# Layer 0's modulation chunks 4 to 11: two weight blocks per step, four column strips together

## The chip, the core and the metric

One core of one Trainium2 chip runs the whole program. The metric is the device time of one execution in microseconds (us). The engines are named as in the profile: PE (TensorE, matmul), PEld (its weight loads), DVE (VectorE), ACT (ScalarE), POOL (GpSimd) and SP (SyncE, which here only issues DMAs). L326 is line 326 of the kernel before.

## The reference

A two-layer transformer trunk in float32 over 512 latent and 256 context tokens of width 1024. Per layer:

```
m  = silu(c) @ w_mod[l] + b_mod[l]          # 6 x 1024 columns, for the latent and the context condition
h  = rmsnorm(x) * g * (1 + m.scale1) + m.shift1
z  = h @ w_in[l]                            # q, k, v, gate u, value v of the gMLP
a  = attention(q, k, v)                     # 8 q heads, 2 kv heads; latent queries see 768 keys, context queries 256
g  = gelu(u) * spatial_mix(layernorm(gelu(v)))
x += m.gate1 * (concat(a, g) @ w_out[l])
x += m.gate2 * (relu(norm2(x) modulated by m.scale2, m.shift2 @ w_ff1[l])**2 @ w_ff2[l])
```

The part that the change touches is the first line for layer 0: two condition vectors (1024 numbers each) times a 1024 x 6144 matrix, in 12 chunks of 512 columns. Chunks 0 to 3 (shift 1 and scale 1) are needed before the first projection; chunks 4 to 11 (gate 1 and the three of the MLP) are needed only after the attention.

## The kernel before, in words

**Layout.** Activations lie feature-major: 128 features on the partitions, tokens along the free axis. Dense products are taken in three passes of fp32r matmuls on a high and a low part of each operand (`split`, L206 to L208: ACT writes the high part, DVE or POOL the low part). The many rows named L203 are all matmuls of the helper `mm`.

**Weight stream.** `block_order` (L120) writes down the order in which weight blocks of 128 x 1024 (512 KB) are used. `pump` (L224) walks this list and issues one DMA per block on SP while fewer than RING = 4 entries are live; `take` hands the oldest entry to its user, and `release` gives the entry back 4100 ns (REL) of the emission clock later. An entry of ordinary weights has a raw buffer (two of these) and a slot in each of two rings of four, "hi" and "lo". A modulation block is not split: it is loaded straight into a "hi" slot, and the "lo" slot that would belong to it stays unused.

**Modulation on PE.** `mod_chunk` (L315) makes one chunk of 512 columns out of 8 matmuls, one per 128 input features k. The stationary operand is `S32[:, k, :]`, 32 columns that repeat the two conditions; the moving operand is 512 columns of a weight block, in plain fp32, which the program runs as two passes (so one matmul is two records of L326). A matmul fills 32 of PE's 128 columns. With NS = 2 (chunks 0 to 3) the products alternate between two column strips; with 4 strips (chunks 4 to 11) feature k goes to strip k % 4, which is rows 32(k % 4) and on of one PSUM bank. A block holds two features, so a block's two matmuls are in strips 0 and 1 or in strips 2 and 3. The generator yields after each block. At the end DVE turns the bank (L334), and four small matmuls (L339) add the strips.

**Attention of layer 0.** `attention` runs first over the context queries (16 tiles of 128 queries of one head), then over the latent queries (32 tiles). A tile is: scores on PE into a `pa` bank (L203 `pa<-B,B`), maximum on DVE (L825), exponential on ACT (L828), transposes on PE (L844), copies of these by ACT (L846) and DVE (L847), and per two tiles the product with V (L203 `pb<-A,B`, 12 matmuls for latent tiles).

**Fillers.** After each tile's scores are emitted, `Flow.step` emits one piece of other PE work, the filler. In layer 0 the fillers are, in order: the pieces of chunks 4 and 5; then a mix of the first half of the output projection ("o" pieces, one of 8 output tiles x 2 token parts of 384, 12 matmuls each) and chunks 6 to 11 ("m" pieces, one weight block each) in the order of the string FILL0; then the second half of the output projection (`proj4(("out", l, 1), ...)`): 8 pieces of 12 matmuls over the 256 context tokens, which need the context heads, and 8 pieces of 12 matmuls over the 512 latent tokens, which need all heads. While the heads for a pass are not all emitted, that generator says "wait" and the step emits nothing.

**Order.** Two things set the order of work. `Flow` keeps an emission clock (`fl.vt`, in ns); what is put off (the transposes by T0, the V products by PV0, the freeing of ring entries by REL) is emitted when the clock gets there. A planner then orders each engine's instructions: of those that are ready in its plan, the one emitted first goes first. A row of matmuls that was emitted together can therefore be cut by an earlier-emitted piece of attention that becomes ready in between. Each engine runs its list strictly in order. In the first stage (`start`) PE and DVE keep the written order.

Of the kernel before, what the change touches and what calls it, by code (L numbers as in the profile page):

```python
# [16 lines left out]
KT = 8  # L17
# [8 lines left out]

# columns of the packed constants
PK1 = {"c": (0, 8), "cc": (8, 16), "bmod": (16, 112), "ng": (112, 144), "gn": (144, 152), "ident": (152, 280), "sel": (280, 312)}
PK2 = {"qg": (0, 64), "kg": (64, 128), "bs": (128, 640)}


# emission lags and periods, in ns of tensor-engine time
PAR = {"KF": 1, "XO": 1, "MS": 3, "KB": 6, "S0": 200.0, "S2": 1.0, "BK": 1, "CS": 0, "S1": 2400.0, "NS": 2, "CX": 0,
# [6 lines left out]


def once(fn):
    """fn, but for the first call alone"""
    left = [fn]
    return lambda: left.pop()() if left else None


class Flow:
    """Emission clock: counts tensor-engine time and emits put-off work once its turn has come."""

# [35 lines left out]
    def fill0(self, until):  # L86
        """pass the time without fillers"""
        while self.vt < until:
            self.vt = max(self.vt, min([until] + [e[0] for e in self.todo]))
            self.tick()  # L90

    def step(self):
        """one piece of filler"""
        while self.fillers:
            try:
                if next(self.fillers[0]) != "wait":
                    break
                return
            except StopIteration:
                self.fillers.pop(0)  # L100
        self.tick()

    def drain(self):
        """Emit everything put off, with fillers in between."""
        while self.todo:
            self.fill(self.todo[0][0] + 1e-6)
# [5 lines left out]

# how pieces of the output projection (o) and of the modulation (m) alternate beside the attention of layer 0
FILL0 = "oooooooommmommmmmmmmmommmmommmommmomoomo"
EARLY = [f"A{i}" for i in range(7, 3, -1)] + [f"B{i}" for i in range(7)] + ["C0", "C1"] + [f"A{i}" for i in range(7, 3, -1)]
# [4 lines left out]
def block_order():  # L120
    o = []
    mod = lambda j: [("mod", 0, j, kb) for kb in range(4)]
    tok = lambda l, g: [("tok", l, g, kb) for kb in range(2)]
# [37 lines left out]
def trunk(ctx: ExitStack, tc: tile.TileContext, xT, pk1, pk2, rope, wsT, w_mod, w_tok, w_u, w_out, w_ff1, w_ff2, outT):  # L161
# [47 lines left out]

# [1 line left out]
    order = block_order()  # L211
# [7 lines left out]
    def convert():  # L219
        """split the oldest block that is held back"""  # L220
        if held:
            split(*held.pop(0))

    def pump():  # L224
        while state["live"] < RING and state["pos"] < len(order):
# [10 lines left out]
            if early:  # L236
                raw = unit(early, [128, 1024], F32)
            elif key[0] == "mod":
                raw = ring.tile([128, 1024], F32, tag="hi", name=nm("hi"), bufs=RING)
            else:  # L240
                raw = ring.tile([128, 1024], F32, tag="raw", name=nm("raw"), bufs=2)
            nc.sync.dma_start(raw, src)
            if key[0] == "mod":
                ready.append((key, raw, None))
                state["pos"] += 1
                state["live"] += early is None
                continue
# [26 lines left out]
    def rsqrt(v, n):  # L274
        """1/sqrt of a small positive tile: a bit estimate, a quadratic and a cubic step."""
        yi = small(n, I32)
# [12 lines left out]

# [1 line left out]
    c1 = const.tile([128, 312], F32, name="c1")  # L291
# [9 lines left out]

    # silu of both conditions
    sc = const.tile([128, 8, 2], F32, name="silu")
# [11 lines left out]
    def mod_chunk(l, j, lag=1200.0):  # L315
        """512 columns of the modulation of both conditions, four partial sums at a time in the four
        32-column strips of the tensor engine; yields between weight blocks."""
        ps = pb()
        ns = PAR["NS"] if j < 4 else 4
        rows = ns * 32  # L320
        for kb in range(4):
            w = take("mod", l, j, kb)[0]
            for k2 in range(2):
                k = kb * 2 + k2
                q = (k % ns) * 32
                pe.matmul(ps[q:q + 32, :], S32[:, k, :], w[:, k2 * 512:(k2 + 1) * 512], start=k < ns, stop=k >= KT - ns)  # L326
            fl.vt += 490.0
            if l or j > 3:
                release()
            if kb < 3:  # L330
                yield
        # 32 by 32 blocks turned, then the strips added
        tr = (tw if l == 0 and j < 4 else tsm)([128, 512])
        vec.transpose(tr[0:rows], ps[0:rows])  # L334

        def fin():
            p4 = pt((128, 4, 2))
            for a in range(4):
                pe.matmul(p4[a * 32:a * 32 + 32], P1("sel")[0:rows], tr[0:rows].rearrange("p (m a i) -> p a m i", m=4, a=4)[:, a, :, 0:2], start=True, stop=True)  # L339
            mod_store(l, j, p4)  # L340
        if lag:
            fl.defer(lag, fin)
        else:
            fin()
        yield

    def mod_wide(l):
        """The modulation of one layer on the vector engine; yields after each half of a weight block."""
        raw = tk([128, 2, 512], F32)
# [6 lines left out]
        for j in range(12):  # L356
            acc = unit("C1", [128, 2, 512], F32)
            for k in range(KT):
# [15 lines left out]
                if k not in PAR["YK"]:  # L374
                    yield
            # sums over the partitions: 32 by 32 blocks turned and summed, then the four strips added
            part = small(32).rearrange("p (c b) -> p c b", c=2)
# [32 lines left out]

# [1 line left out]
    class Norm:  # L412
# [17 lines left out]
        def sums(self, *others):  # L430
            """1/rms of each token, for other chunks in the same go"""
            every = (self,) + others
# [50 lines left out]

# [1 line left out]
    class TokProj:  # L485
# [14 lines left out]
        def bank(self, tp):  # L500
            """256 tokens"""
            ps = (pt if self.early else pb)((128, 2, 256))
# [13 lines left out]
        def wide(self, ks=range(KT)):  # L516
            """the first 512 tokens, feature block by feature block as they come"""
            if 0 in ks:
# [11 lines left out]

# [1 line left out]
    DENSE = {0: ((0, 384), (384, 384)), 1: ((0, 512),)}  # L532
# [17 lines left out]
    def consts(l):  # L550
        k2 = const.tile([128, 640], F32, tag="k2", name=nm("k2"))
        nc.scalar.dma_start(k2, pk2[l])
        P2 = lambda k: k2[:, PK2[k][0]:PK2[k][1]]
        # rope tables times the gains
        cs = tw([128, 2, 4, 32])
        nc.scalar.dma_start(cs, rope)
        G = const.tile([128, 2, 2, 4, 64], F32, tag="G", name=nm("G"))
        for i, nme, s in ((0, "qg", HD ** -0.5), (1, "kg", 1.0)):
            g = P2(nme).rearrange("p (a b) -> p a b", a=2)
            vec.tensor_scalar_mul(g, g, s)  # L560
            for hf in range(2):
                gb = lambda a: g[:, a, :].unsqueeze(1).broadcast_to([128, 4, 32])
                vec.tensor_tensor(out=G[:, i, 0, :, hf * 32:hf * 32 + 32], in0=cs[:, 0], in1=gb(hf), op=ALU.mult)
                vec.scalar_tensor_tensor(out=G[:, i, 1, :, hf * 32:hf * 32 + 32], in0=cs[:, 1], scalar=(-1.0, 1.0)[hf], in1=gb(1 - hf), op0=ALU.mult, op1=ALU.mult)
        # spatial gating
        wr = ring.tile([128, 512], F32, tag="raw", name=nm("raw"), bufs=2)
# [9 lines left out]
    def layer(l, h, nxt, K, kv=None, kv0=0):  # L576
# [11 lines left out]
        def qk(ps4, tp, nh, which):  # L588
            """ps4 [128, 2, nh, 64] -> normed and rotated."""
            sq = tsm([128, 2, nh, 64])  # L590
# [28 lines left out]
        def turn(stk, tp, plan):  # L619
            """plan: (destination, [(head in stack, first column)]) -> transposes of both token tiles."""  # L620
            for dst, hs in plan:
# [46 lines left out]
        with region('kv%d' % l):  # L668
            kv.wide(range(kv0, KT))
        # gate path u, feature-major, twice its gelu  # L670
        U = [unit(f"C{i}", [128, 2, T], F32) for i in range(2)]
# [13 lines left out]
        def u_part(m, part):  # L685
            """one token part of a gate tile: first the noised tokens, later the context"""
            off, n = ((0, SEQ), (SEQ, CTX))[part]
# [89 lines left out]

        # residual update: x += gate * product, by condition
        def gate(i, m, off, n, src):
# [6 lines left out]
        def proj4(keys, R, i, passes, bank, post=None, gates=None):  # L786
            """keys: 4 blocks; passes: lists of token parts, each over all 8 output tiles."""
            wbs = {}
# [22 lines left out]

        # attention; the split output of a head pair takes the place of its queries
        def attn_tile(j, blk, hh, qt, st):
# [132 lines left out]

        # squared-ReLU MLP
        hslots = [f"B{i}" for i in range(7)] + ["C0"]
# [14 lines left out]
        def ff1_first():  # L963
            """first chunk, one token part after the other, while the other part is being normed"""
            wbs = [take("ff1", l, m) for m in range(4)]
# [197 lines left out]
```

## Time and profile before

| | |
|---|---|
| three runs | 1532.07, 1532.15 and 1535.47 us, median 1532.15 |
| profiled execution, first to last instruction (span) | 1530.9 us |
| what lies around the span | 1.25 us against the median run; the profiled execution has no other time of its own |
| PE busy | 1484.1 us, 97% of the span |
| DVE, ACT, POOL busy | 957.4, 682.6, 402.0 us |
| mean granted TensorE clock | 0.993 |
| matmuls of chunks 4 to 11 | first at 176.6 us, last at 341.0 us |
| context tiles, latent tiles of layer 0 | about 176 to 227 us, 227 to 345 us |
| first matmul of the first MLP product | 381.7 us |

Times are from the start of the span. "Busy" is the time covered by at least one instruction of the engine; matmuls are pipelined and their ends are modelled, so neighbouring matmul records overlap. In the timeline, a row gives the start, the time that the merged instructions cover, the engine, the line, the tiles (out<-in) and the count.

### The profile page before, as it was taken

How to read it: one execution, taken by the hardware profiler on the slowest of the kernel's cores; microseconds unless marked ns; L12 is line 12 of the kernel's file. 1: busy time of each engine (PE TensorE's matmuls, PEld its weight loads, DVE VectorE, ACT ScalarE, POOL GpSimd, SP SyncE). 2: the span in 40 equal slices, each digit the busy share in tenths (PEclk: the TensorE clock that was granted, in tenths of full speed). 3: DMA queues.
4: the chain of work that ended last, by engine and by line, in shares of the span. 5: the costliest groups of instructions: out<-in, count | busy, mean ns of one | idle time of the engine just before them, and what ended most of it. 6: DMA issues, size and time to landing. Idle time of an engine off the chain costs nothing.

```text
span 1530.9 us, 22786 instructions
## 1 busy us (share of the span) xinstructions
PE 1484.1 (97%) x8804; PEld 1321.5 (86%) x8804; DVE 957.4 (63%) x1874; ACT 682.6 (45%) x1142; POOL 402.0 (26%) x362
## 2 busy tenths in 40 slices
PE   6999899999999999999999999998999999999998
PEld 2899686779899999999999998996889888888887
DVE  5868966776855555555555547988796644444443
ACT  3542355564545453545444424535784433322221
POOL 0112320023244545545454603035213000000000
PEclk9999999999999999999999999999999999999999
DMA  9221324321134333333333321221101333332332
GB/s 359 67 74 48 119 91 152 110 83 56 62 108 122 113 123 126 111 118 106 124 109 124 98 68 56 86 80 44 41 1 56 97 96 97 98 97 97 96 98 79
DMA packets 49948, 148.83 MB, mean 97 GB/s; under 512 B 5424, under 2 KB 6832, under 8 KB 49840
## 3 DMA queue, kind: packets, MB, share of 16 engines
q1 hardware_dynamic: 49264, 146.46, 29.9%
q8 instruction: 69, 1.13, 0.3%
q10 hardware_dynamic: 576, 0.92, 0.2%
q14 instruction: 39, 0.32, 0.1%
HBM read 145.26 MB, written 2.10 MB: 96 GB/s over the span
## 4 chain that ended last, share of the span: by engine, by line
PE 82%; DVE 12%; DMA 2%; ACT 2%; issue 1%; POOL 0%; SPq 0%; ACTq 0%; POOLq 0%; DVEq 0%
PE pa L203 51%; PE pb L203 21%; PE pt L844 3%; PE pt L203 3%; PE pb L326 2%; DVE lo L208 1%; DMA X<-in_xT 1%; DMA C<-in_w_mod 1%; DVE X L784 1%; DMA A<-in_w_mod 1%; DVE m L277 1%; PE pt L626 1%; DVE B L961 1%; ACT hi L207 1%; PE pb L865 0%
## 5 line engine op out<-in xcount | busy, mean ns | idle before, releaser
L203 PE MATMUL pa<-A,hi 128*128 128x384 f32 (+2 forms) x1696 | 449.2, 347 | 1.7 <-ACT w L954 0.6
L207 ACT CAST hi<-raw 128x1024 fp32r<-128x1024 f32 x171 | 179.5, 1050 | 409.9 <-PE pa L203 326.3
L208 DVE TENSOR_TENSOR lo<-raw,hi 128x1024 fp32r<-128x1024 f32 x155 | 202.7, 1308 | 215.8 <-ACT hi L207 212.4
L203 PEld LDWEIGHTS pa<-A,hi 128*128 128x128 f32 x1696 | 304.7, 188 | 25.9 <-ACT w L954 1.8
L369 POOL TENSOR_TENSOR C<-C,s 128x512 f32<-128x512 f32 x168 | 240.5, 1463 | 245.0 <-ACT s L368 244.8
L203 PE MATMUL pa<-A,lo 128*128 128x384 f32 (+2 forms) x848 | 293.4, 347 | 1.1 <-DVE lo L208 1.1
L203 PE MATMUL pa<-B,hi 128*128 128x384 f32 (+1 forms) x900 | 246.4, 356 | 4.4 <-DVE X L784 4.4
L203 PEld LDWEIGHTS pa<-B,hi 128*128 128x128 f32 x900 | 162.9, 188 | 21.5 <-DVE X L784 9.2
L784 DVE SCALAR_TENSOR_TENSOR X<-pa,modT,X 128x384 f32<-128x384 f32 (+1 forms) x168 | 88.0, 547 | 143.0 <-PE pa L203 143.0
L203 PEld LDWEIGHTS pa<-A,lo 128*128 128x128 f32 x848 | 159.3, 188 | 12.0 <-DVE lo L208 1.3
L203 PE MATMUL pa<-B,lo 128*128 128x384 f32 (+1 forms) x450 | 158.1, 353 | 0.0
L203 PE MATMUL pb<-B,hi 128*128 128x256 f32 (+2 forms) x600 | 152.3, 340 | 0.4 <-DVE X L784 0.4
L368 ACT ACTIVATE s<-k,silu 128x512 f32<-128x512 f32 x168 | 114.3, 716 | 49.4 <-DMA k<-in_w_mod 27.3
L203 PE MATMUL pb<-hi,A 128*128 128x256 f32 x672 | 126.1, 285 | 0.0
L784 DVE SCALAR_TENSOR_TENSOR X<-pb,modT,X 128x512 f32<-128x512 f32 (+3 forms) x116 | 69.1, 602 | 75.8 <-PE pb L203 75.3
L203 PEld LDWEIGHTS pb<-B,hi 128*128 128x128 f32 x600 | 104.0, 189 | 11.6 <-DVE X L784 1.0
L203 PEld LDWEIGHTS pb<-hi,A 128*128 128x128 f32 x672 | 106.1, 191 | 0.2 <-issue 0.2
L203 PE MATMUL pb<-B,lo 128*128 128x256 f32 (+2 forms) x300 | 101.5, 338 | 0.0
L203 PE MATMUL pb<-lo,A 128*128 128x256 f32 x336 | 95.3, 284 | 0.0
L203 PEld LDWEIGHTS pa<-B,lo 128*128 128x128 f32 x450 | 84.4, 188 | 5.8
L847 DVE TENSOR_TENSOR A<-pt,A 128x384 fp32r<-128x384 f32 (+1 forms) x144 | 73.6, 535 | 16.4 <-ACT A L846 14.4
L846 ACT CAST A<-pt 128x384 fp32r<-128x384 f32 (+1 forms) x144 | 64.6, 469 | 43.3 <-PE pt L844 39.5
(169 smaller groups left out, 2300.3 us busy)
## 6 DMA issues: line engine op xcount, KB each, us to landing
raw<-in_w_ff SPq DMA_DIRECT2D x128, 512.0 KB, 3.5
k<-in_w_mod SPq DMA_DIRECT2D x96, 256.0 KB, 3.0
hi<-in_w_mod SPq DMA_DIRECT2D x32, 512.0 KB, 3.6
raw<-in_w_tok SPq DMA_DIRECT2D x19, 512.0 KB, 3.5
raw<-in_w_out SPq DMA_DIRECT2D x16, 512.0 KB, 3.5
A<-in_w_mod SPq DMA_DIRECT2D x8, 512.0 KB, 9.9
raw<-in_w_u SPq DMA_DIRECT2D x8, 512.0 KB, 3.5
B<-in_w_mod SPq DMA_DIRECT2D x6, 512.0 KB, 10.2
```

The source lines that it names most:

```text
L203: pe.matmul(out, a, b, start=start, stop=stop)
L207: act.copy(hi, src)
L208: (eng or vec).tensor_tensor(out=lo, in0=src, in1=hi.bitcast(F32), op=ALU.subtract)
L277: vec.tensor_scalar(yi, v.bitcast(I32), -0.5, 1595932665.0, op0=ALU.mult, op1=ALU.add)
L326: pe.matmul(ps[q:q + 32, :], S32[:, k, :], w[:, k2 * 512:(k2 + 1) * 512], start=k < ns, stop=k >= KT - ns)
L368: act.activation(p, w, AF.Copy, scale=s)
L369: pool_e.tensor_tensor(out=a, in0=a, in1=p, op=ALU.add)
L626: pe.transpose(p[:, o:o + 128], stk[:, t, hh, c0:c0 + 128].bitcast(F32), ident)
L784: vec.scalar_tensor_tensor(out=xs, in0=src[:, s - off:e - off], scalar=modT[l][:, i * 8 + m, cond:cond + 1], in1=xs, op0=ALU.mult, op1=ALU ...
L844: pe.transpose(tp_[:, (kt - k0) * 128:(kt - k0) * 128 + 128], p[:, kt * 128:kt * 128 + 128], ident)
L846: act.copy(pth[:, k0:k0 + step, d], src)
L847: vec.tensor_tensor(out=ptl[:, k0:k0 + step, d], in0=src, in1=pth[:, k0:k0 + step, d].bitcast(F32), op=ALU.subtract)
```

## The change

Chunks 4 to 11 take their weights two blocks at a time. One ring entry now holds two blocks, the first in the "hi" slot and the second in the "lo" slot, each by its own 512 KB DMA. A piece of `mod_chunk` is four matmuls, in strips 0 to 3, and a chunk has two pieces instead of four. The emission clock counts 260 ns for each matmul (1040 for four) where it counted 490 for a block of two; chunks 0 to 3 keep their two strips and one block per piece, but count 520. FILL0 has 12 "m" (one per pair of blocks) instead of 24, and the same 16 "o".

```diff
-FILL0 = "oooooooommmommmmmmmmmommmmommmommmomoomo"
+FILL0 = "oooooooomomomomomomomomommmm"
...
-    mod = lambda j: [("mod", 0, j, kb) for kb in range(4)]
+    mod = lambda j: [("mod", 0, j, kb) for kb in range(0, 4, 1 if j < 4 else 2)]
...
             elif key[0] == "mod":
-                raw = ring.tile([128, 1024], F32, tag="hi", name=nm("hi"), bufs=RING)
+                two = [ring.tile([128, 1024], F32, tag=t, name=nm(t), bufs=RING) for t in ("hi", "lo")]
+                for i in range(2):
+                    nc.sync.dma_start(two[i], w_mod[0, key[2], key[3] + i])
+                ready.append((key, *two))
+                state["pos"] += 1
+                state["live"] += 1
+                continue
...
             if key[0] == "mod":
                 ready.append((key, raw, None))
                 state["pos"] += 1
-                state["live"] += early is None
                 continue
...
         ns = PAR["NS"] if j < 4 else 4
         rows = ns * 32
-        for kb in range(4):
-            w = take("mod", l, j, kb)[0]
-            for k2 in range(2):
+        for kb in range(0, 4, ns // 2):
+            ws_ = take("mod", l, j, kb)[:ns // 2]
+            for k2 in range(ns):
                 k = kb * 2 + k2
-                q = (k % ns) * 32
-                pe.matmul(ps[q:q + 32, :], S32[:, k, :], w[:, k2 * 512:(k2 + 1) * 512], start=k < ns, stop=k >= KT - ns)
-            fl.vt += 490.0
-            if l or j > 3:
+                q = k2 * 32
+                pe.matmul(ps[q:q + 32, :], S32[:, k, :], ws_[k2 // 2][:, k2 % 2 * 512:(k2 % 2 + 1) * 512], start=k < ns, stop=k >= KT - ns)
+            fl.vt += PAR["MV"] * ns
+            if j > 3:
                 release()
-            if kb < 3:
+            if kb < 4 - ns // 2:
                 yield
```

`PAR` gains `"MV": 260.0`. Comments are taken out elsewhere, and nothing else changes.

2 rows, old and new, of the table PAR are left out of this document.

## The prediction

> **What bounds the kernel now.** I read the page first, then each engine's busy time by stage, then PE's rows of the stage in which chunks 4 to 11 run.
>
> ```profile
> span 1530.9 us, 22786 instructions
> PE 82%; DVE 12%; DMA 2%; ACT 2%; issue 1%; POOL 0%; SPq 0%; ACTq 0%; POOLq 0%; DVEq 0%
> ```
>
> PE holds 82% of the chain that ended last.
>
> ```profile
> core 0: us, PE busy (x) PEld busy (x) DVE busy (x) ACT busy (x) POOL busy (x), PEclk, DMA share, GB/s
> 176.00:227.00 51.00, 43.60 (x277) 34.36 (x275) 35.25 (x97) 26.74 (x72) 15.81 (x22) 0.93 0.41 136
> 187.00:193.00 6.00, 5.46 (x18) 2.98 (x16) 3.14 (x12) 2.19 (x8) 0.57 (x3) 0.53 0.05 21
> 227.00:345.00 118.00, 116.43 (x739) 83.01 (x737) 83.09 (x175) 67.89 (x150) 17.73 (x36) 1.00 0.35 112
> 345.00:364.00 19.00, 18.97 (x158) 18.73 (x157) 10.68 (x24) 8.58 (x20) 7.69 (x8) 1.00 0.17 56
> 364.00:382.00 18.00, 18.00 (x84) 14.74 (x83) 13.42 (x28) 6.94 (x12) 6.08 (x4) 1.00 0.17 59
> 1098.00:1140.00 42.00, 41.80 (x307) 37.98 (x305) 39.74 (x85) 37.45 (x87) 7.62 (x23) 1.00 0.00 1
> 1140.00:1150.00 10.00, 9.47 (x75) 8.61 (x73) 7.43 (x17) 6.30 (x16) 1.30 (x4) 1.00 0.01 2
> ```
>
> The context tiles of layer 0 are the first row, the latent tiles the third, what follows them the fourth and fifth. From 227 us on PE is covered 99% of the time, DVE 70%, ACT 58%. So a microsecond taken from PE between 227 and 382 us comes off the end, as long as another engine doesn't take PE's place. The context stage has 7.4 us in which PE is idle. The last two rows are layer 1's latent tiles without any filler, and what follows them; they serve below.
>
> **What the modulation costs.** The row is that of L326 from 176 to 382 us; the other rows are PE's timeline.
>
> ```profile
> L326 PE MATMUL pb<-hi,S 128*32 128x512 f32 x128 | 36.6, 612 | 0.9 <-DMA hi<-in_w_mod 0.9
> ```
>
> ```profile
> 227.80 1.05 PE L326 MATMUL pb<-hi,S 128*32 128x512 f32 x4
> ...
> 267.08 1.07 PE L326 MATMUL pb<-hi,S 128*32 128x512 f32 x8
> 268.08 0.55 PE L844 MATMUL pt<-c,w 128*128 128x128 f32 x3
> ...
> 283.94 1.04 PE L326 MATMUL pb<-hi,S 128*32 128x512 f32 x2
> 284.92 1.69 PE L203 MATMUL pb<-A,B 128*128 128x256 f32 x12
> 286.54 1.04 PE L326 MATMUL pb<-hi,S 128*32 128x512 f32 x2
> 287.52 0.96 PE L203 MATMUL pa<-B,B 128*128 128x512 f32 x4
> ...
> 340.99 1.05 PE L326 MATMUL pb<-hi,S 128*32 128x512 f32 x4
> ```
>
> A matmul is two records. At 283.94 one matmul alone holds PE for 0.98 us, until the next row starts at 284.92. At 267.08 four matmuls (two blocks that happened to meet, in strips 0 to 3) hold it for 1.00 us. One, two and four strips cost the same: the price is per group, 1.0 us. A group covers about 1.05 us, so the 36.6 us are 35 groups, for 64 matmuls. Sixteen full groups of four would do.
>
> The pair 283.94 and 286.54 is one block torn in two: after its first matmul a product with V, emitted earlier, had become ready and the planner put it between. From 227.80 to 340.99 there are 96 records in 28 groups: 15 of two matmuls, 11 of one, one of three, one of four. So 12 matmuls lost their partner, which is 6 torn blocks of 24, 0.25 per joint between two matmuls of a block.
>
> **The sum.** It is made against the span of 1530.9 us; the median run of 1532.15 is 1.25 us above it, and I carry this over unchanged.
>
> *Groups removed.* A group of four has three joints. With no tears there are 16 groups, 19 fewer: -19 us. With 0.25 tears at each joint there are 12 tears, 28 groups, 7 fewer: -7 us. A tear lets the waiting work through, so the next joint is less exposed than the first; but a piece of four also holds PE longer in the plan. I take the middle, 7 tears and 23 groups: 12 fewer, -12 us. One of these stood before 182 us, ahead of this idle stretch, where PE time is free:
>
> ```profile
> 186.64 0.69 PE L844 MATMUL pt<-c,w 128*128 128x128 f32 x2 [4.75 <-ACT w L828]
> ```
>
> That leaves -11 us, with ends -18 and -6.
>
> The four-strip price is a row of this kernel, but the Trainium skill speaks against it: "TensorE: Matmul & The Clock Gate", section "Part 3: Packing small matmuls — row/col tiling", gives 2.38 times for three column tiles, not 3. At that efficiency (0.79) a group of four would take 0.98/0.79 = 1.24 us, an estimate from that page, and the sixteen pieces would give back up to 3.8 us. The row at 267.08 (1.00 us) doesn't agree, and I go by the row.
>
> *Steps of filler.* There are 48 attention tiles and one piece per tile. Before, 8 pieces of chunks 4 and 5 plus 40 of FILL0 make exactly 48, and the second half's context pieces come behind the last tile. Now there are 4 + 28 = 32. So tiles 33 to 40 get the 8 context pieces of the second half, and tiles 41 to 48 get nothing ("wait"). PE's work is the same; its place is not.
>
> Bare tiles: the trace has them in layer 1. These are the exponentials, one per tile, from 227 to 345 and from 1098 to 1140 us.
>
> ```profile
> L828 ACT ACTIVATE w<-pa,m 128x768 f32<-128x768 f32 x31 | 28.1, 907 | 12.3 <-DVE m L825 10.6 <-DVE A L395 1.5
> L828 ACT ACTIVATE w<-pa,m 128x768 f32<-128x768 f32 x18 | 16.4, 910 | 1.2 <-DVE m L825 1.2
> ```
>
> Bare tiles take 42.0/18 = 2.33 us, with PE busy 2.32 and DVE 2.21 of it. So DVE stands just behind PE. In layer 0 DVE also makes the low part of the attention output, which layer 1 gives to POOL, and that could lift a tile to DVE's pace. I count 1 us for the eight tiles; the ends are 0 and 4 (0.5 us each).
>
> *The tail.* The eight context pieces covered the wait for the last tile.
>
> ```profile
> 347.77 0.40 PE L203 MATMUL pb<-B,hi 128*128 128x256 f32 x2
> ...
> 353.53 5.75 PE pb L203 x48
> ...
> 357.69 1.60 PE L203 MATMUL pb<-A,B 128*128 128x256 f32 x12
> ...
> 364.13 0.63 PE L203 MATMUL pb<-B,hi 128*128 128x512 f32 x2
> ```
>
> Matmuls over 256 columns go at 5.75/48 = 0.12 us, so the 96 of the context pieces are 11.5 us of the 16.4 between 347.77 and 364.13, where the latent pieces start. Without them PE waits for exponential, transposes, copies and V product. Layer 1 again shows that case:
>
> ```profile
> 1139.45 0.71 PE L203 MATMUL pa<-B,B 128*128 128x512 f32 x3
> ...
> 1148.45 0.49 PE L203 MATMUL pb<-B,hi 128*128 128x256 f32 x2
> ```
>
> From the last scores (ended 1140.16) to the second half 8.3 us pass, and PE is covered for 9.47 of the 10 us from 1140. Transposes and V products of the tiles before fill nearly all of it. I take 2 us lost (ends 0.5 and 11.5, all of the cover).
>
> *Weights.* The DMAs stay 32 of 512 KB for these chunks, now two per entry on SP's queue.
>
> ```profile
> hi<-in_w_mod SPq DMA_DIRECT2D x32, 512.0 KB, 3.6
> SPq L242 <- PE pb L326: 92.0, 22, 10.8
> PE pb L326 <- DMA hi<-in_w_mod: 0.9, 1, 0.9
> L207 ACT CAST hi<-raw 128x1024 fp32r<-128x1024 f32 x171 | 179.5, 1050 | 409.9 <-PE pa L203 326.3
> L208 POOL TENSOR_TENSOR lo<-raw,hi 128x1024 fp32r<-128x1024 f32 x4 | 9.6, 2394 | 5.5 <-ACT hi L207 5.5
> ```
>
> SP waits for PE to free slots, PE hardly for the data (0.9 us, once). Four entries now hold eight blocks, so a pair is fetched at least two steps (over 6 us) ahead of its use. If that cover were gone, a pair would cost PE about 3.6 us plus the second block's time; with all 16 pairs that is over 58 us, which I exclude because the slots free no later than before. Behind a waiting pair on SP stand the output blocks. The second half's four blocks are now wanted at tile 33, and each gets its slot from one of the last four pairs; after the slot it needs the cast (1.05 us) and the low part (2.39 us on POOL). The first has one slot freed at tile 29, so it is ready; if not, PE stands for at most 3.4 us. I count 0. In exchange the first half's blocks find free slots sooner in the context stage, which could fill up to 3 us of its idle time. Also 0.
>
> *Emission clock.* Chunks 0 to 3 add 30 ns 16 times in a stage with written order, and lags there are relative to later calls; 0, with a bound of 2 us either way for what the planner reshuffles. Vector transposes (L334) and strip sums (L339) stay eight each. Half as many releases cost no engine time.
>
> Sum: -11 + 1 + 2 = -8 us, so 1522.9 for the span and **1524.0** for the run.
>
> **The rivals.**
>
> *The groups stay whole.* Nearly every group in the timeline directly follows a tile's scores, so all four may be ready at once with nothing else pending. At most 2 tears: -17 or so, plus 2 for the tail: 1517. Against it speak the 6 torn blocks of 24.
>
> *The groups are torn as before* (the change doesn't do what it says). 28 groups or more, -6 after the hidden one, plus 3 for bare tiles and tail: -3, 1529, no measurable difference. For it: 0.25 tears per joint, three joints now.
>
> *The tail is bare.* One mechanism: the last tile's chain isn't shortened by the pieces' going, and PE idles 11.5 us before the latent pieces. An idle stretch also costs clock: after the 4.75 us of idle before 186.64 the granted clock was 0.53 from 187 to 193 us, a loss of 6 x 0.47 = 2.8 us. Together 14.3 against a saving of at most 11: about 3 us slower by that, and with 28 groups (-6) 8 us slower; I name 1538. It decides once PE loses more behind the last scores than the groups saved. Against it: 8.3 us and full clock at the same place in layer 1. The same page of the Trainium skill ("Why this matters for your kernels") warns of idle gaps over about 3 us between bursts of matmuls; the row of 187 to 193 us agrees, that of 1140 shows no such gap.
>
> **How the numbers follow.** Forecast (saving of 5 to 12 us) 0.46; groups whole 0.17; torn as before 0.21; bare tail 0.16. About 0.3% (4.6 us) is what a measurement can tell from no change. Faster: 0.46 + 0.17 = 0.63; same 0.21; slower 0.16. The likeliest case alone spans 1520 to 1527. For 8 in 10 the range goes down to 1515 (no tears, and 2 us gained in the context stage) and up to 1536 (the tail bare with 23 groups: 1532.15 - 11 + 14.3 = 1535.5); it leaves out a bare tail with torn groups.
>
> **What would show it.** L326's busy time from 176 to 382 us falls from 36.6 to about 24 us (23 groups; 17 if whole, 29 if torn), most groups x8. No L326 in the last 16 tiles, context pieces of the second half among the tiles, the last eight exponentials about 2.4 us apart. PE's idle time between the last scores and the latent pieces: about 2 us, clock at 1.00. First MLP product at about 373 instead of 381.7 us, and everything behind it shifted by as much. Wrong would be: groups mostly x4 and x2, a wait of PE for weights at tile 33, a clock under 0.9 after the last scores, or a gain that is gone again at 400 us.

## The result and the profile after

The changed kernel takes 1517.01 us (median of four runs, 1516.59 to 1518.99) against 1533.07 us of the kernel before on the same chip (four runs, 1532.07 to 1535.47): a ratio of 0.9896, 95% interval 0.9885 to 0.9908. That is 16 us saved where 8 were forecast. Line numbers of the changed kernel are 6 higher from the modulation on (L326 became L332, L844 became L850, L828 became L834).

The first rows are of the page: the span, and the chain that ended last, by engine.

```profile
span 1514.8 us, 22788 instructions
...
PE 79%; DVE 12%; ACT 3%; DMA 3%; issue 1%; POOL 0%; SPq 0%; ACTq 0%; DVEq 0%; POOLq 0%
```

The span is 16.1 us shorter. Next come busy times by stage. The columns are the stretch, its length, and the busy time of PE, PEld, DVE, ACT and POOL with the instruction counts; then the granted clock.

```profile
core 0: us, PE busy (x) PEld busy (x) DVE busy (x) ACT busy (x) POOL busy (x), PEclk, DMA share, GB/s
176.00:228.00 52.00, 44.98 (x296) 34.57 (x295) 37.24 (x91) 25.87 (x68) 18.87 (x22) 0.93 0.48 173
228.00:324.00 96.00, 94.47 (x717) 79.57 (x716) 74.02 (x160) 59.55 (x133) 22.18 (x36) 1.00 0.35 116
324.00:340.00 16.00, 14.34 (x105) 12.79 (x103) 13.02 (x29) 11.87 (x27) 1.51 (x7) 1.00 0.01 2
340.00:347.00 7.00, 4.38 (x33) 3.52 (x31) 5.77 (x13) 5.08 (x12) 0.39 (x2) 1.00 0.00 0
347.00:366.00 19.00, 19.00 (x94) 15.99 (x95) 12.87 (x29) 7.10 (x13) 5.22 (x3) 1.00 0.19 55
```

The context stage (first row) keeps its idle time of PE: 7.0 us of 52, before it was 7.4 of 51. The third and fourth rows are new: between 324 and 347 us, the bare tiles and the wait for the last one, PE is idle for 1.7 and 2.6 us, together 4.3. The clock there is 1.00.

The timeline of PE shows the groups, and where the stages now lie.

```profile
185.10 1.07 PE L332 MATMUL pb<-hi,S 128*32 128x512 f32 x2 [5.58 <-DVE w L611]
185.12 1.07 PE L332 MATMUL pb<-lo,S 128*32 128x512 f32 x2
...
186.81 1.91 PE L332 MATMUL pb<-hi,S 128*32 128x512 f32 x2
188.66 0.52 PE L850 MATMUL pt<-c,w 128*128 128x128 f32 x2
188.93 0.48 PE L203 MATMUL pa<-B,B 128*128 128x256 f32 x2
189.35 0.62 PE L332 MATMUL pb<-hi,S 128*32 128x512 f32 x1
...
278.48 0.62 PE L332 MATMUL pb<-hi,S 128*32 128x512 f32 x2
278.50 0.62 PE L332 MATMUL pb<-lo,S 128*32 128x512 f32 x2
278.94 0.60 PE L332 MATMUL pb<-hi,S 128*32 128x512 f32 x2
278.95 0.60 PE L332 MATMUL pb<-lo,S 128*32 128x512 f32 x2
279.48 0.88 PE L850 MATMUL pt<-c,w 128*128 128x128 f32 x6
...
285.24 0.61 PE L871 MATMUL pb<-c,rc 128*128 128x128 f32 x4
285.78 0.62 PE L332 MATMUL pb<-hi,S 128*32 128x512 f32 x2
...
338.65 0.61 PE L871 MATMUL pb<-c,rc 128*128 128x128 f32 x4
339.10 0.82 PE L850 MATMUL pt<-c,w 128*128 128x128 f32 x6
...
347.12 0.63 PE L203 MATMUL pb<-B,hi 128*128 128x512 f32 x2
...
366.19 0.40 PE L203 MATMUL pa<-A,hi 128*128 128x256 f32 x2
```

A group of four strips (278.48) is eight records, two from each block and pass, and holds PE until 279.48: 1.00 us. The whole trace has 19 groups: 16 pieces, three of them torn, each behind its first matmul (the first tear is at 186.81, its rest at 189.35). The second half's latent pieces start at 347.12 instead of 364.13, and the first MLP product at 366.19 instead of 381.66. So 15.5 of the 16.1 us are there by the first MLP product.

Two things hide in these rows. The four L871 matmuls last 0.54 us when a modulation group follows (285.24 to 285.78) and 0.45 when transposes follow (338.65 to 339.10): a group also costs 0.09 us at its entry, charged to the row ahead of it. And after the idle stretch of 5.58 us a piece takes 1.71 us (185.10 to 186.81), since the clock is low there.

The modulation matmuls alone, as the time covered by them (in the view by stretches), and what PE waited for in the stage (waits: total, times, longest):

```profile
170.00:382.00 212.00, 21.67 (x128) 3.17 (x128) 0.98 0.31 105
```

```profile
PE pt L850 <- DVE A L853: 5.9, 7, 1.5
PE pb L332 <- DVE w L611: 5.6, 1, 5.6
```

PE does not wait for modulation weights anywhere in the stage; the wait of 0.9 us that it had before is gone.

**Where the 16 us come from.** Each PE record is charged with the time to the next record's start, less what the trace calls idle; this is done from the first context scores to the first MLP product (205.4 us before, 190.3 after, 15.1 less).

| us | before | after | difference |
|---|---|---|---|
| modulation matmuls | 34.4 | 20.6 | -13.8 |
| entry of a group, on the rows ahead | 3.5 | 1.6 | -1.9 |
| scores, products with V, transposes, without entries | 85.1 | 81.6 | -3.5 |
| PE idle | 9.0 | 12.8 | +3.8 |
| everything else | 73.3 | 73.7 | +0.4 |

The entry is the difference between the matmul ahead of a group and the median of its kind and shape; it is booked against the third row of the table, where nearly all these matmuls are. The first two rows are the change as argued, the fourth is its price. The third was not forecast.

About half of the third row is the clock behind the idle stretch of the context stage. Before, scores and transposes ran there; two score matmuls took 0.78 us at 188.59, where two took 0.48 after the change, at 188.93 and full clock (PE's timeline before):

```profile
188.59 0.78 PE L203 MATMUL pa<-B,B 128*128 128x256 f32 x2
...
189.91 1.92 PE L326 MATMUL pb<-hi,S 128*32 128x512 f32 x2
```

The rows of attention had 3.7 us at a clock near 0.5 before and 0.3 after, since modulation matmuls stand in that place now. By an estimate (time times the missing share of the clock) this is 1.7 us of the 3.5, while the modulation's own loss grew from 1.0 to 1.9 us. What made the other 1.8 us is open.

### The profile page after: what moved, and what is told of

It is laid out like the page before. It is cut to its first block, busy times and chain, and to the rows that moved or that the text cites. A ratio compares the mean times of both kernels' runs of the same rounds, so it can differ in the third digit from the quotient of the medians.

```text
span 1514.8 us, 22788 instructions
## 1 busy us (share of the span) xinstructions
PE 1463.9 (97%) x8804; PEld 1316.3 (87%) x8804; DVE 959.7 (63%) x1874; ACT 682.4 (45%) x1142; POOL 403.5 (27%) x362
## 4 chain that ended last, share of the span: by engine, by line
PE 79%; DVE 12%; ACT 3%; DMA 3%; issue 1%; POOL 0%; SPq 0%; ACTq 0%; DVEq 0%; POOLq 0%
PE pa L203 51%; PE pb L203 20%; PE pt L203 3%; PE pt L850 3%; DVE lo L208 1%; PE pb L332 1%; ACT hi L207 1%; DMA raw<-in_w_tok 1%; DMA B<-in_w_mod 1%; DMA A<-in_w_mod 1%; DVE m L283 1%; DVE B L967 1%; DVE m L831 1%; ACT w L834 1%; DVE A L853 1%
## 5 line engine op out<-in xcount | busy, mean ns | idle before, releaser
L203 PEld LDWEIGHTS pa<-A,lo 128*128 128x128 f32 x848 | 159.3, 188 | 12.3 <-DVE lo L208 1.5
L434 POOL TENSOR_TENSOR acc<-acc,s 128x256 f32<-128x256 f32 (+1 forms) x43 | 47.0, 1092 | 138.7 <-ACT s L432 138.2
L834 ACT ACTIVATE w<-pa,m 128x768 f32<-128x768 f32 (+1 forms) x80 | 65.7, 821 | 38.2 <-DVE m L831 29.8
```

The lines of the kernel that those rows point to most:

```text
L203: pe.matmul(out, a, b, start=start, stop=stop)
L434: eng.tensor_tensor(out=self.acc, in0=self.acc, in1=sq, op=ALU.add)
L834: act.activation(p, ps[:, 0:nk], AF.Exp, bias=nmx, accum_out=sm)
```

## The experiments

"Own" is the time that the modulation matmuls hold PE, counted as in the table above; "idle" is that of its fourth row. Each ratio is taken against runs of the kernel before beside it on the same chip (medians 1532.3 to 1533.4 us).

| kernel | us | ratio to before, 95% | own | idle |
|---|---|---|---|---|
| before | 1533.07 | | 34.4 | 9.0 |
| the change | 1517.01 | 0.9896 [0.9885, 0.9908] | 20.6 | 12.8 |
| two strips | 1532.54 | 0.9995 [0.9985, 1.0004] | 35.9 | 11.7 |
| one strip | 1553.32 | 1.0134 [1.0119, 1.0150] | 59.0 | 9.9 |
| pieces untorn | 1515.70 | 0.9886 [0.9872, 0.9901] | 18.6 | 12.8 |
| context pieces last | 1522.47 | 0.9931 [0.9917, 0.9946] | 21.1 | 14.2 |
| fillers spread | 1521.28 | 0.9924 [0.9908, 0.9941] | 26.3 | 8.7 |
| spread and untorn | 1511.95 | 0.9864 [0.9849, 0.9879] | 18.2 | 9.4 |
| one block per ring entry | 1521.97 | 0.9928 [0.9913, 0.9943] | 22.6 | 12.4 |
| the same, clock of before | 1522.17 | 0.9935 [0.9923, 0.9948] | 22.6 | 12.3 |
| shared ring entry alone | 1529.57 | 0.9980 [0.9971, 0.9990] | 34.1 | 8.5 |
| the same, changed clock | 1530.57 | 0.9987 [0.9978, 0.9996] | 33.9 | 8.7 |
| changed clock alone | 1531.86 | 1.0000 [0.9991, 1.0009] | 36.0 | 8.2 |
| the change, clock of before | 1516.93 | 0.9901 [0.9887, 0.9914] | 20.6 | 12.4 |

**Does the saving come from four strips at once?** The theory says that the number of PE groups sets the time; the rival says that it is the staging (fewer steps, paired DMAs). Both kernels keep the staging of the change and take strips away.

```diff
+        sn = ns if j < 4 else 2          # the second kernel: 1
-        rows = ns * 32
+        rows = sn * 32
-                q = k2 * 32
+                q = k2 % sn * 32
-                pe.matmul(..., start=k < ns, stop=k >= KT - ns)
+                pe.matmul(..., start=k < sn, stop=k >= KT - sn)
```

> The changed kernel with one edit: the four matmuls of a piece go to two strips instead of four (first and third to strip 0, second and fourth to strip 1), so a piece is two groups by construction; ring entries, pieces, FILL0 and clock stay. Theory (the gain is the smaller number of groups, 1.0 to 1.1 us of PE each): about 18 groups more than the changed kernel's 19, so +18 to +20 us, 1535 to 1537, no gain left over the kernel before. Rival (the gain comes from fewer filler steps and a deeper prefetch, not from the groups): stays near 1517 to 1520.

> As the run with two strips, but all four matmuls of a piece go to one strip: 64 groups. Theory: 45 groups more than the changed kernel at 1.0 us or a little more each, +45 to +49, 1562 to 1566, and the slope per group is the same as with two strips. Rival (PE time of the modulation is partly hidden): the slope falls well below 1.0 us per group, under 1550.

With two strips the time is that of before, with one strip it is 20 us longer. Against the change, own time rises by 15.3 and 38.4 us, and the run by 15.5 and 36.3. So the strips carry the saving. Both runs came out lower than expected by my price of 1.0 us a group. PE's timeline shows why, first with two strips, then with one:

```profile
271.95 1.05 PE L333 MATMUL pb<-hi,S 128*32 128x512 f32 x4
272.83 1.03 PE L333 MATMUL pb<-lo,S 128*32 128x512 f32 x4
273.79 0.97 PE L203 MATMUL pa<-B,B 128*128 128x512 f32 x4
```

```profile
322.99 1.90 PE L333 MATMUL pb<-hi,S 128*32 128x512 f32 x4
324.73 1.88 PE L333 MATMUL pb<-lo,S 128*32 128x512 f32 x4
326.54 0.88 PE L851 MATMUL pt<-c,w 128*128 128x128 f32 x6
```

Two groups in a row take 1.84 us, four take 3.55. A group that another follows costs only about 0.87 us (1.74 for the two from 322.99 to 324.73); the rest of the 1.0 and the 0.09 of entry are paid once per visit.

**What do the tears cost?** In the first kernel matmuls 2 to 4 of a piece are emitted with priority and ordered behind the first.

```diff
-                pe.matmul(ps[q:q + 32, :], S32[:, k, :], ws_[k2 // 2][...], ...)
+                with tc.high_priority() if j > 3 and k2 else nullcontext():
+                    one = pe.matmul(ps[q:q + 32, :], S32[:, k, :], ws_[k2 // 2][...], ...)
+                if j > 3 and k2:
+                    tc.add_manual_dep(one, first, NoSync)
+                elif j > 3:
+                    first = one
```

> The changed kernel, with matmuls two to four of a piece raised in the planner's order and made to follow the first, so that no piece is torn: 17 groups instead of 19. Theory (1.0 us of PE per group): -2 to -3 us, 1514 to 1515. Rival (three torn pieces cost nothing, because what came between had to run anyway and PE idles elsewhere): 1517.

One tear of three is left, own time falls by 2.0 us (1.0 per tear), the run by 1.3, which lies between the two expectations. The own time confirms the price of a tear; the run's gain alone would not, since its interval overlaps that of the change.

**What do bare tiles and the tail cost?** One kernel takes the cover from eight more tiles by holding back the context pieces; another adds empty steps, so that fillers last to the end (a dot emits nothing).

```diff
-FILL0 = "oooooooomomomomomomomomommmm"          # fillers spread
+FILL0 = "oooooooomo.mo.mo.mo.mo.mo.mo.mo.m..m..m..m.."
...
-gates = [lambda: done[1] == 4, lambda: done[0] == 8]     # context pieces last
+gates = [lambda: done[0] == 8] * 2
```

> The changed kernel, but the context pieces of the second half also wait for the last head, so tiles 33 to 48 are all bare and the pieces cover the last tile's chain. Same groups. Theory A (the 4.3 us of idle PE at the end come from the uncovered chain of the last tile): 1513 to 1515. Theory B (they come from bare tiles, where DVE paces): sixteen bare tiles instead of eight, 1517 to 1521.

> The changed kernel with FILL0 stretched by 16 empty steps ("oooooooo" + "mo." eight times + "m.." four times, a dot being a tile without filler), so that the 32 pieces fill all 48 tiles and the context pieces of the second half stand behind the last tile again. Its planned order of PE has 9 pieces torn after their first matmul instead of 3. Theory (a group costs PE 1.0 us, the bare end costs about 4 us of idle PE): 6 groups more, +6, and the idle time between 324 and 347 us back, -4: about 1519. Rival (the bare end cost nothing, the planner's reordering decides): 1523 or more; rival (tears cost nothing): 1513.

Held back, the run is 5.5 us longer than the change, above the ranges of both theories. Twelve of its bare tiles lie here (the kernel with context pieces last, by stretches):

```profile
297.00:330.00 33.00, 29.73 (x207) 25.63 (x207) 27.99 (x60) 25.22 (x57) 2.84 (x12) 1.00 0.01 2
```

PE is idle for 3.3 us of 33, 0.27 us per tile, and no other engine is full (DVE 85%, ACT 76%). Of the 3.3 us, 2.3 are transposes that wait for a copy by DVE. So the tiles seem to go at the pace of short waits between the engines, not of one of them; no run tests that. My bound for a bare tile was 0 to 0.5 us, my value 0.12. Idle time and own time explain 1.9 of the 5.5 us; scores, products with V and transposes held PE 3.2 us longer.

Spread out, the tail is covered (fillers spread, then spread and untorn, by stretches):

```profile
324.00:347.00 23.00, 22.77 (x182) 20.06 (x181) 16.95 (x37) 14.82 (x34) 5.72 (x9) 1.00 0.14 46
```

```profile
324.00:347.00 23.00, 22.91 (x173) 21.45 (x172) 13.30 (x29) 10.53 (x26) 4.99 (x9) 1.00 0.00 1
```

Idle time falls by 4.1 us, as hoped, and yet the run is 4.3 us longer than the change, 2 us above the expectation: the planned order now has nine torn pieces, and own time rises by 5.7. If tears are to blame, the same order without them must be the best kernel.

> Both: the stretched FILL0 and untorn pieces, 17 groups. Theory: -2 for the groups and -4 for the covered end against the changed kernel, 1510 to 1512. If only the tears count: 1514 to 1515; if only the end: 1513; if neither: 1517.

It is: 1511.95 us, 5 us under the change and 21 under before, with an interval that lies apart from that of the change. The two edits together give more than the sum of each (-1.3 and +4.3), because the second removes what the first provokes.

**The last 3 us.** The table above leaves 3.5 us in scores, V products and transposes, of which the clock explains about half. The suspects for the rest were the shared ring entry and the emission clock. One kernel keeps pieces of four but gives each block its own entry; one keeps pieces of one block, in the steps of before, and shares the entry.

```diff
-                two = [ring.tile([128, 1024], F32, tag=t, ...) for t in ("hi", "lo")]     # one block per entry
+                raw = ring.tile([128, 1024], F32, tag="hi", ...)
...
-            ws_ = take("mod", l, j, kb)[:ns // 2]
+            ws_ = [take("mod", l, j, kb + i)[0] for i in range(ns // 2)]
...
-        for kb in range(0, 4, ns // 2):            # shared entry alone
+        for kb in range(4):
+            if j < 4 or kb % 2 == 0:
+                ws_ = take("mod", l, j, kb)
+            w = ws_[0 if j < 4 else kb % 2]
```

> The changed kernel's pieces of four matmuls, clock and FILL0, but the ring of before: one block per entry, in the hi slot alone, and a piece takes two entries. Theory (two blocks in one slot only matter because they bring four matmuls together, PE hardly waits for data): same groups within two or three, 1517 to 1520. Rival (the deeper prefetch of the shared slot is needed): PE waits for the second block of most pieces, some 2 us each, 1530 or more.

> The other half alone: two blocks share one ring entry as in the changed kernel, but pieces are one block of two matmuls, with FILL0 and the clock of before. Theory: about 35 groups as before, so no change, 1531 to 1535. Rival (prefetch depth or ring order gives part of the gain): 1524 to 1529.

Without shared entries the saving is 5 us smaller, more than the 0 to 3 expected; with shared entries alone there is a small gain where none was expected. In the kernel with one block per entry PE waited for weights, and the idle stretch of before comes after it (waits of PE):

```profile
PE pt L845 <- ACT w L829: 4.3, 1, 4.3
...
PE pb L327 <- DMA hi<-in_w_mod: 1.4, 1, 1.4
```

Its modulation has 21 groups in place of 19 (+2.0 us of own time). To see whether these differences are only the luck of one planned order, the emission clock was moved on its own, in four kernels.

```diff
-            fl.vt += 490.0                         # before, and the shared entry alone
+            fl.vt += 520.0
...
-       "MV": 260.0                                # the change, and one block per entry
+       "MV": 245.0
```

> The kernel before with one edit: a step of the modulation counts 520 ns of the emission clock instead of 490, which is what the change does to it. Work, ring and pieces are those before; only the planned order of the rows shifts a little (34 lists of modulation matmuls instead of 33). Theory (the ring entry of two blocks is what gave the last 3 us of the saving, the emission clock gave nothing): 1532 to 1535 us, within 0.1% of before. Rival (a small shift of the emission clock reorders the rows of the context stage, and that alone is worth about 3 us, in the change as in the kernel with the shared ring entry): 1529 to 1531, or as much slower, 1535 to 1537.

> The changed kernel with the emission clock of before: 245 ns per matmul (490 per two, 980 per four) instead of 260. The planned order keeps the 17 lists of modulation matmuls and the three cut pieces. Theory (the clock is worth nothing): 1516 to 1518.5 us. Rival (reordering in the context stage is worth 3 us either way): 1514 or less, or 1520 and more.

> Two blocks per ring entry and pieces of one block, with 520 ns per step in place of 490: the earlier kernel with the shared ring entry alone, with another emission clock. If the ring entry gives the 3 us by itself, this too lies 2.5 to 4.5 us under before (1528.5 to 1531). If what was seen there was the luck of one planned order, it can lie anywhere from 1528 to 1536, and as far from the ring kernel as the clock alone moves before.

> Pieces of four matmuls with one block per ring entry, as in the earlier kernel with single entries (1522.0), with 245 ns per matmul instead of 260. 21 lists of modulation matmuls as there. Ring theory: again 4 to 5 us above the changed kernel, 1520.5 to 1522.5. Rival (luck of one planned order): the distance to the changed kernel is another, 1516 to 1520 or over 1524.

The clock is worth nothing: 1.0000 in the kernel before, 1516.93 against 1517.01 us in the changed one. And the effect of the ring stays under either clock: without shared entries 5.0 and 5.2 us more than the change, with them alone 0.2 and 0.13% less than before (3.1 and 2.0 us). So the shared entry is worth 2 to 3 us with small pieces and 5 with large ones. Counted as in the table above, the stage of the kernel with one block per entry is 4.2 us longer than that of the change: own time is 2.0 us more, entries 1.2, everything else 1.0, and scores, V products and transposes only 0.4, while idle time is 0.4 less in spite of the wait for weights. With pieces of four the effect of the shared entry therefore does not show in the third row. With small pieces that row is 2.8 us below before, but with the clock alone changed it is 1.0 us below and the run is the same, so that row can move by about 1 us without a gain. How the entry gives its 2 to 3 us there is not settled, and neither is the rest of the third row.

## Why the prediction was right in its direction and off by half in its size

**The price per group** was right at full clock: 1.00 us for four strips (278.48, and the pieces that follow it). The Trainium skill ("TensorE: Matmul & The Clock Gate", "Part 3: Packing small matmuls — row/col tiling"), by whose 2.38 times for three tiles a piece would have taken 1.24 us (an estimate), does not hold for this shape: the groups at 278.48 and after took 1.00. What the price lacked was the entry of 0.09 us, which I left in the rows ahead: 33 entries became 17, and 1.9 us went with them.

**The groups** are the step that failed. I counted 0.25 tears per joint and gave a piece of four three joints: 7 tears, 23 groups, -12 us. There were 3 tears in 16 pieces, all at the first joint. Before, 7 of the 32 blocks were torn (0.22 per piece), now 3 of 16 (0.19): a tear goes with the piece, not with the joint. A waiting piece of attention got in behind the first matmul or not at all. The kernel with fillers spread shows the same place, nine times, but nine tears of 16, so the rate is that of one planned order and not a constant. I had named the reason ("A tear lets the waiting work through, so the next joint is less exposed than the first") and still took the middle. The time covered by these matmuls fell from 36.62 to 21.67 us, where I had named 24 (17 if whole, 29 if torn). The sum also started one group too high: the trace before has 34 groups (six up to 200 us, 28 behind), not 35, because the division by 1.05 counted the matmul at 189.91, which covers 1.92 us at the slow clock, nearly twice. So 15 groups were saved. At 0.98 us they are 14.7, and they gave 13.8 us of own time, mostly because two of the groups left fall in the slow clock behind the idle stretch: 1.71 us for a whole piece (185.10) and 1.85 for one matmul (186.81), 1.6 us over the price, where one group was 0.9 over it before. The stretch in the view by stretches, with a granted clock of 0.52:

```profile
185.00:189.00 4.00, 3.90 (x13) 0.90 (x13) 3.73 (x14) 1.07 (x3) 1.13 (x2) 0.52 0.20 29
```

**The hidden group.** The idle stretch in the context stage did not go away, but the stage's idle time as a whole did not grow (7.4 to 7.0 us). The stretch starts earlier and lasts 5.58 instead of 4.75 us; what PE waits for there is behind a long row of DVE, in its timeline:

```profile
178.26 5.59 DVE L781 TENSOR_TENSOR A<-C,A 128x768 fp32r<-128x768 f32 x2
```

**Bare tiles and tail** were named with their place and clock, and came to 4.3 us where I had counted 1 + 2. In ACT's timeline the exponentials of the tiles without filler:

```profile
325.65 0.90 ACT L834 ACTIVATE w<-pa,m 128x768 f32<-128x768 f32 x1 [0.32 <-DVE m L831]
...
334.68 0.91 ACT L834 ACTIVATE w<-pa,m 128x768 f32<-128x768 f32 x1
...
338.59 0.90 ACT L834 ACTIVATE w<-pa,m 128x768 f32<-128x768 f32 x1 [1.63 <-DVE m L831]
...
343.20 0.90 ACT L834 ACTIVATE w<-pa,m 128x768 f32<-128x768 f32 x1 [0.22 <-DVE m L831]
```

Four intervals take 9.03 us, 2.26 each, where 2.4 was forecast; the interval to 338.59 takes 3.9 and the last one, to 343.20, takes 4.6. The tail itself lost 2.6 us (340 to 347), between my ends of 0.5 and 11.5 and far from the rival that called it bare. PE's longest idle stretch there is the one in this row of its timeline (the 1.5 us among the waits above ends at 291.5), and the clock stayed at 1.00:

```profile
343.69 0.55 PE L850 MATMUL pt<-c,w 128*128 128x128 f32 x3 [1.03 <-DVE A L853]
```

**Weights and ring** were put at 0, with a gain of up to 3 us in the context stage as a bound. The pairs are not late. The gain exists: 2 to 5 us by the runs. It doesn't come as less idle time in the context stage, as I had argued; of the 5 us with large pieces, 2.0 are two groups fewer, which I had not thought of.

**Emission clock**: 0 forecast, 0 measured, within 1.4 us either way (the interval).

**The rivals.** "The groups stay whole" named 1517 us. Its condition was at most 2 tears, and there were 3; its tail was too cheap by 2 us and its saving lacked the entries and the rows of attention, and these cancel. Its time was hit by luck, its sum was not. "Torn as before" and "the tail is bare" are refuted by the 19 groups and by the 4.38 busy microseconds of PE in the 7 from 340 us. The likeliest case's own 1520 to 1527 did not hold the time; the range to 1515 did.

In the forecast's own terms: groups -13.8 and entries -1.9 (forecast -11 for both), bare tiles, tail and the rest of the idle time +3.8 (forecast +3), rows of attention -3.5 (forecast 0), everything else +0.4; that is -15.1 by the first MLP product, but for rounding. So of the 7 us beyond the forecast, 4.7 are the groups with their entries and 3.5 the rows of attention, which the forecast held at nothing, less 1.2 us for idle time and everything else.

## What to carry to other kernels

Count the visits of a small matmul to PE, not the matmuls: four column strips at once cost what one costs, so pieces should be as wide as the strips allow, and whatever is emitted as a piece should be kept together in the planned order. When fillers become fewer, spread them until the last bare stretch is covered, and look again at the tears, since here spreading alone lost 4 us and spreading with untorn pieces won 5. Price an operation by the time to the next row's start and compare the row ahead of it with its like elsewhere: a cost that sits in the neighbour is easily missed.

## What the runs showed of the hardware beyond that

- A modulation group that another follows directly costs about 0.87 us (3.55 us for four in a row, 1.84 for two), one that stands between full-width matmuls 1.00 plus 0.09 on the row ahead. The Trainium skill ("TensorEngine Tiling (Array Packing)", "Key Properties") says that changing the tiling mode drains TensorE; the rows agree with that, at about 0.2 us per visit, though no run here separates the drain from other causes.
- Four matmuls of a piece run at once only as far as they have strips of their own: 1.00 us for four strips, 1.84 for two, 3.55 for one.
